# Stick-breaking attention: weights copied by a transfer within SBUF into rounded float32 tiles and transposed in that format

## Chip, cores and metric

The kernel runs on one core of a Trainium2 chip. The metric is the device time of one execution in microseconds (us); the number given for a kernel is the median of its runs.

## What is computed

One decoder layer over 1024 tokens of width 1024: a modulated RMS norm, one input projection, two attention families side by side (a sparse one with compressed, selected and windowed keys, and a stick-breaking one), their gated merge with an output projection, and a squared-ReLU MLP. The change lies in the stick-breaking family alone. It has 8 heads of width 64, no softmax, and is strictly causal:

```python
z = einsum('bqhd,bshd->bhqs', qb, k) * scale
mask = key_pos[None, :] < t[:, None]
log_keep = where(mask, log_sigmoid(-z), 0.0)
suffix = cumsum(log_keep, axis=3, reverse=True) - log_keep
a = where(mask, exp(log_sigmoid(z) + suffix), 0.0)
out = einsum('bhqs,bshd->bqhd', a, v)
```

So a weight is sigmoid(z) times the product of sigmoid(-z) over all keys between it and the query.

## The kernel before

The layer runs in stages on one core: norm and first projections, sparse attention, stick-breaking attention, the up-projections with merge and output projection, then the MLP. Products that need accuracy are split in a high and a low part in the rounded float32 format (F32R), and the parts are multiplied apart. All matrices that the attention stages leave room for are multiplied inside them: `fill_all` (L1044) yields the matmuls of 28 units of the input projection (L761, 128 x 512 each), and `drive` (L1067) lets the attention code, written as generators, run and puts in fill matmuls by an estimated cost. `behind` (L746) ties every sixth fill matmul behind the last attention matmul. 96 fill matmuls are kept back (`TAIL`, L1042) and run right after the stick-breaking stage. The final order on each engine is made by a scheduler from this program order. All transfers of the stage are issued by one engine, SP, in order.

`sb_gens` (L1089) is the stick-breaking stage. For each of 8 heads there are three groups of four blocks (`chunks_of`, L1140): kind 0 are the query rows 0 to 3 (of 128 queries each) with keys up to the diagonal, 512, 384, 256 and 128 wide; kind 1 rows 4 to 7 with the last 512 keys; kind 2 the same rows with the keys before those, again 512, 384, 256 and 128 wide. That makes 96 blocks.

- `sb_a` (L1148) computes a block's scores on TensorE (PE) in a PSUM bank of a ring of three (`psx`, L1156 to L1159), then two sigmoids on ScalarE (ACT): sigmoid(z) into an SBUF tile (`sig` by width, two of each, or `sigr` for kind 1, five; L1160, L1161), sigmoid(-z) in place in the bank (L1162). Its second half `fin` runs the products from the right by a scan on VectorE (DVE) into `Pt` (L1171) and multiplies `sig` with them on GpSimd (POOL, L1173).
- `turn` (L1180) transposes the finished weights on PE, up to four 128 x 128 pieces from up to four tiles into one bank of a ring of two (`pt`, L1188). In the program text a group's turns stand beside the next group's scores; the scheduler lets the scores run up to three groups ahead.
- `halves` (L1192) splits the transposed bank: the high part by a copy on ACT (`th`, L1196), the low part by a subtraction on DVE (`tl`, L1197).
- `times_v` (L1200) multiplies both with the head's value rows into one bank (`po`, L1208). At the end of a row group the two halves are added and stored (`osum`, L1214, and L1215 by SP).
- `prep` (L1104) splits the next head's keys and queries, mostly on POOL in pieces of 1 to 2.4 us; `prep_v` (L1120) transposes value rows (L1126) for two heads at a time.
- Beside all that, one step of another matrix, `ada_rest` (L427), runs on ACT and POOL after every second block in the first heads: a load by SP (L436), a scaling on ACT (L456) and an addition on POOL (L460).

The sparse stage already has the step that the change brings here: `scaler` (L910) scales a block on POOL, SP copies it into an F32R tile `Pr` (L926, L927), and L975 transposes from there with the F32R identity `identr`.

Of the kernel before, what the change touches and what calls it, by code (L numbers as in the profile page):

```python
# [6 lines left out]
F32 = mybir.dt.float32  # L7
F32R = mybir.dt.float32r
# [7 lines left out]
S = 1024  # L16
# [19 lines left out]
def build(tc, I, out):  # L36
    nc = tc.nc
    opened = []

    def pool(name, side=None, bufs=1, **kw):  # L40
        if side:
            kw.update(side=side, reuse_waits="tile")
        p = tc.alloc_tile_pool(name=name, bufs=bufs, **kw)
        opened.append(p)
        return p
# [9 lines left out]
    f = lambda t: t.bitcast(F32)  # L55
# [29 lines left out]
    z_d = dr.tile([28, 128, S], F32, name="z_d")  # L85
# [11 lines left out]
    def psx(name="psx"):  # L97
        return ps.tile([128, 512], F32, tag="s", bufs=3, name=name)

    def pt(name="pt"):  # L100
        return ps.tile([128, 512], F32, tag="t", bufs=2, name=name)
# [6 lines left out]
    ident = const.tile([128, 128], F32, name="ident")  # L108
# [633 lines left out]
    def track(ins):  # L742

        last[:] = [ins.ins]
# [29 lines left out]
    identr = wu.tile([128, 128], F32R, name="identr")  # L774
# [314 lines left out]
    def sb_gens(sp):  # L1089
# [7 lines left out]
            return zr  # L1097

        def load_v(p):
            vr = sp.tile([128, S], F32, name="vr", bufs=1)  # L1100
            nc.sync.dma_start(vr, z_d[8 + p])
            return vr

        def prep(h, ld):  # L1104
# [15 lines left out]
        def prep_v(vr, V):  # L1120
            tv = [sp.tile([128, NT, 2, HD], F32R, name="V", bufs=3) for _ in range(2)]
            for q in range(2):
                p = pt()
                for c in range(4):
                    kt = q * 4 + c
                    track(nc.tensor.transpose(p[:, c * 128:(c + 1) * 128], vr[:, kt * 128:(kt + 1) * 128], ident))  # L1126
                yield 4 * PT_
                pv_ = p.rearrange("p (c h d) -> p c h d", c=4, h=2)
                for j in range(2):
                    nc.scalar.copy(tv[j][:, q * 4:q * 4 + 4, 0], pv_[:, :, j])  # L1130
                for j in range(2):
                    nc.vector.tensor_tensor(tv[j][:, q * 4:q * 4 + 4, 1], pv_[:, :, j],
                                            f(tv[j])[:, q * 4:q * 4 + 4, 0], op=OP.subtract)
                yield 0.0
            V.extend(tv)
# [12 lines left out]
        def sb_a(kind, chunk, ops, A, edges):  # L1148

            i, c0, c1 = chunk  # L1150
            Q, Kh, Kl = ops
            w = c1 - c0
            p = psx()
            qs = Q[:, i * 128:(i + 1) * 128]
            diag = kind != 2
            track(nc.tensor.matmul(p[:, :w], qs, Kh[:, c0:c1], start=True, stop=False))  # L1156
            track(nc.tensor.matmul(p[:, :w], qs, Kl[:, c0:c1], start=False, stop=not diag))
            if diag:
                track(nc.tensor.matmul(p[:, w - 128:w], identr, diagr, start=False, stop=True))  # L1159
            sig = sp.tile([128, w], F32, name="sigr" if kind == 1 else "sig%d" % w, bufs=5 if kind == 1 else 2)  # L1160
            nc.scalar.activation(sig, p[:, :w], AF.Sigmoid, scale=HD ** -0.5)  # L1161
            nc.scalar.activation(p[:, :w], p[:, :w], AF.Sigmoid, scale=-(HD ** -0.5))  # L1162
            A[i, kind] = (sig, c0)

            def fin():
                Pt = sp.tile([128, 640], F32, name="Pt", bufs=6)
                if diag:
                    nc.vector.memset(Pt[:, w:w + 1], 1.0)
                else:
                    nc.vector.tensor_copy(Pt[:, w:w + 1], edges.pop(i)[:, 0:1])  # L1170
                nc.vector.tensor_tensor_scan(Pt[:, 0:w][:, ::-1], p[:, 0:w][:, ::-1], zero.to_broadcast([128, w]),  # L1171
                                             1.0 if diag else Pt[:, w:w + 1], op0=OP.mult, op1=OP.add)
                nc.gpsimd.tensor_tensor(sig, sig, Pt[:, 1:w + 1], op=OP.mult)  # L1173
                if kind == 1:
                    edges[i] = Pt
            return fin, max(w, 256) * 2 / 2400.
# [3 lines left out]
        def turn(h, g, kt, A):  # L1180

            p = pt()
            c0 = max(0, kt - 4 * g) * 128
            for i in range(max(4 * g, kt), 4 * g + 4):
                o = (i - 4 * g) * 128
                sig, s0 = [A[i, x] for x in ((0,) if g == 0 else (1, 2)) if (i, x) in A and
                           A[i, x][1] <= kt * 128 < A[i, x][1] + A[i, x][0].shape[1]][0]
                track(nc.tensor.transpose(p[:, o:o + 128], sig[:, kt * 128 - s0:kt * 128 - s0 + 128], ident))  # L1188
            turned.append((h, g, kt, c0, p))
            return (512 - c0) / 128. * PT_  # L1190

# [26 lines left out]
        def sb_all():  # L1218
            lds = {0: (load(0, 0), load(4, 0))}
            vr = load_v(0)  # L1220
            ops = {}
            for r in prep(0, lds[0]):
                ops[0] = r
            V = []
            for c in prep_v(vr, V):
                yield c
# [3 lines left out]
            for k in range(len(groups) + 1):  # L1230
                if k < len(groups):
                    h, kind = groups[k]
                    if kind == 0:
                        A[h, 0] = {}
                        if h + 1 < 8:
                            lds[h + 1] = (load((h + 1) // 2, h + 1), load(4 + (h + 1) // 2, h + 1))
                            if h % 2 == 1:
                                vr = load_v((h + 1) // 2)
                    if kind == 1:
                        A[h, 1] = {}  # L1240
                        if h + 1 < 8:
                            extra.append(prep(h + 1, lds[h + 1]))
                            if h % 2 == 1:
                                extra.append(prep_v(vr, V))
                    chunks = chunks_of(kind)
                for c in range(4):
                    cost = 0.0
                    if k < len(groups):
                        fin, cost = sb_a(kind, chunks[c], ops[h], A[h, min(kind, 1)], edges)
                        late.append(fin)  # L1250
                        yield cost
# [4 lines left out]
                    if k > 0:  # L1256
                        hb, kb = groups[k - 1]
                        g = min(kb, 1)
                        cost += turn(hb, g, (3, 7, 3)[kb] - c, A[hb, g])

                        if split_ and (wait[0] or split_[0][2] != 4 * split_[0][1] + 3):
                            while len(split_) > 0:
                                cost += times_v(V)
                            wait[0] = 0
                        elif split_:
                            wait[0] = 1
                        if len(turned) > 1:
                            halves()
# [62 lines left out]
    def col_sums(r, bank):  # L1331
        acc = L["wr"].tile([128, D], F32, name="raw", bufs=3)
        nc.sync.dma_start(acc, acc_d[r])
        p = bank()
        for j in range(NK):
            nc.tensor.matmul(p[:, j:j + 1], acc[:, j * 128:(j + 1) * 128], ones[:, 0:1], start=True, stop=True)
        return p
# [43 lines left out]
    sp = pool("sb", "right")  # L1381
# [49 lines left out]
    for n in range(len(units) + lag):  # L1431
        if n < len(units):
            ma[n] = up_unit(0, n)
        if n >= lag:
            d, th = units[n - lag]
# [7 lines left out]
        if n == 8:  # L1443
            p = col_sums(1, px)
            nc.vector.tensor_tensor(s2, p[:, :NK], cols[:, 24:32], op=OP.add)
        if n == 10:
            p = col_sums(2, px)
# [146 lines left out]
    A, SPL, U = {}, {}, {}  # L1594
# [199 lines left out]
```

## Time and profile before

| | |
|---|---|
| median of 3 runs (lowest to highest) | 1703.29 us (1702.85 to 1706.73) |
| the profiled execution: its own time | 1704.85 us |
| the profiled execution: span, first to last instruction | 1703.1 us |
| mean granted TensorE clock | 0.989 of 2.4 GHz |
| PE busy | 1636.8 us, 96% |
| DVE busy | 1273.8 us, 75% |
| POOL busy | 950.7 us, 56% |
| ACT busy | 873.9 us, 51% |
| DMA, SP's hardware queue | 276.13 MB, 48.8% of 16 engines' span |

The profile shows one execution. Busy time is the time in which an engine had an instruction in work; the ends of PE's pipelined matmuls are modelled, so successive matmuls overlap in the rows and the distance of their starts is the better measure. The chain is followed back from the last instruction: at each step to what released it, or to the instruction before it on its engine. A wait is named by who waited, and for whom.

### The profile page before, as it was taken

To read this page: it belongs to the slowest core of one execution; us is meant where nothing else is said; L and a number is where in the kernel's file an instruction comes from. 1 tells how busy PE (TensorE), PEld (TensorE's weight loads), DVE (VectorE), ACT (ScalarE), POOL (GpSimd) and SP (SyncE) were. 2 spreads that over 40 slices of the span, in tenths; PEclk is the share of its full clock that TensorE was granted. 3 is DMA by queue.
4 is the path that set the end of the run, shared out by engine and by line. 5 is a ranking of instruction groups with operands and counts; after the bars stand their busy time and mean duration, and the time that the engine had idled before them with its cause. 6 is when DMAs were issued, how large, how long until landed. Compare 5 with 4: busy or idle time off the path is not lost.

```text
span 1703.1 us, 25878 instructions
## 1 busy us (share of the span) xinstructions
PE 1636.8 (96%) x8484; PEld 1377.4 (81%) x8484; DVE 1273.8 (75%) x2614; ACT 873.9 (51%) x1898; POOL 950.7 (56%) x837
## 2 busy tenths in 40 slices
PE   6999999999999989999999999989999999999998
PEld 5879888888888867878778887768788888888886
DVE  7698478778777557878655557569888888979897
ACT  6433476667666456766554435534444443454442
POOL 0021143434434268775326303399889897989897
PEclk9999999999999999999999999999999999999999
DMA  9465344444543474441187543855363554636232
GB/s 304 109 198 157 110 142 156 128 149 143 166 131 125 130 196 128 115 125 59 36 301 232 165 151 127 292 212 210 134 262 116 231 211 148 251 113 268 98 148 99
DMA packets 195103, 279.87 MB, mean 164 GB/s; under 512 B 19401, under 2 KB 145049, under 8 KB 186009
## 3 DMA queue, kind: packets, MB, share of 16 engines
q1 hardware_dynamic: 190744, 276.13, 48.8%
q10 hardware_dynamic: 4224, 2.10, 0.4%
q8 instruction: 67, 1.10, 0.3%
q14 instruction: 68, 0.55, 0.1%
HBM read 203.71 MB, written 39.86 MB: 143 GB/s over the span
## 4 chain that ended last, share of the span: by engine, by line
PE 73%; POOL 8%; DMA 6%; DVE 6%; issue 3%; ACT 3%; SPq 1%; POOLq 0%; DVEq 0%; ACTq 0%
PE pd L761 15%; PE psx L1734 10%; PE pd L1668 7%; PE pt L1668 5%; PE px L1357 5%; PE po L955 4%; PE px L1470 4%; PE po L1734 3%; POOL raw L1708 3%; PE pt L975 2%; PE psx L844 2%; DMA adraw<-in_ada_w_dram 2%; PE psx L845 2%; POOL wbl L1710 1%; PE psx L603 1%
## 5 line engine op out<-in xcount | busy, mean ns | idle before, releaser
L1737 DVE TENSOR_TENSOR acc<-acc,psx 128x512 f32<-128x512 f32 x288 | 178.7, 675 | 9.8 <-PE psx L1734 9.7
L761 PE MATMUL pd<-uh,uwh 128*128 128x512 f32 x448 | 181.2, 404 | 0.7 <-ACT zo L1051 0.7
L761 PE MATMUL pd<-ul,uwh 128*128 128x512 f32 x448 | 177.4, 396 | 0.0
L761 PE MATMUL pd<-uh,uwl 128*128 128x512 f32 x448 | 177.1, 395 | 0.0
L66 DVE TENSOR_TENSOR wl<-aw,wh 128x1024 fp32r<-128x1024 f32 x49 | 114.6, 2339 | 63.9 <-ACT wh L61 63.9
L1708 POOL TENSOR_TENSOR raw<-r 128x512 f32<-128x512 f32 x80 | 132.5, 1675 | 32.1 <-ACT r L1643 32.0
L1734 PE MATMUL psx<-wbl,rah 128*128 128x512 f32 x336 | 131.3, 391 | 5.9 <-POOL wbl L1710 4.6
L1734 PE MATMUL psx<-wbh,rah 128*128 128x512 f32 x336 | 130.6, 390 | 1.9 <-ACT wbh L1709 1.5
L1734 PE MATMUL psx<-wbh,ral 128*128 128x512 f32 x336 | 130.9, 390 | 0.1
L947 DVE TENSOR_TENSOR tl<-pt,th 128x512 fp32r<-128x512 f32 (+8 forms) x168 | 103.5, 619 | 32.9 <-ACT th L946 31.4
L946 ACT CAST th<-pt 128x512 fp32r<-128x512 f32 (+8 forms) x168 | 88.9, 533 | 68.2 <-PE pt L975 67.0
L1710 POOL TENSOR_TENSOR wbl<-raw,wbh 128x1024 fp32r<-128x1024 f32 x40 | 108.9, 2724 | 19.5 <-ACT wbh L1709 19.5
L63 POOL TENSOR_SCALAR uwh<-uwr 128x512 fp32r<-128x512 f32 x54 | 34.3, 645 | 136.0 <-PE pd L761 115.9
L1696 POOL TENSOR_TENSOR w<-w,grow 128x1024 f32<-128x1024 f32 x32 | 95.0, 2992 | 11.8 <-DVE aw L1624 11.8
L1709 ACT CAST rah<-raw 128x1024 fp32r<-128x1024 f32 x40 | 41.5, 1051 | 113.9 <-PE po L1734 60.7
L761 PEld LDWEIGHTS pd<-uh,uwl 128*128 128x128 f32 x448 | 84.9, 189 | 17.2
L761 PEld LDWEIGHTS pd<-uh,uwh 128*128 128x128 f32 x448 | 85.2, 190 | 14.9 <-ACT zo L1051 1.1
L901 POOL TENSOR_TENSOR pcx<-pcx,tot 128x64 f32<-128x64 f32 (+7 forms) x32 | 11.5, 359 | 153.5 <-ACT Pn L864 40.8
L761 PEld LDWEIGHTS pd<-ul,uwh 128*128 128x128 f32 x448 | 85.1, 190 | 14.0
L1668 PE MATMUL pd<-mth,wh 128*128 128x512 f32 x224 | 87.3, 390 | 0.9 <-ACT wh L61 0.9
L1668 PE MATMUL pd<-mth,wl 128*128 128x512 f32 x224 | 87.1, 389 | 0.9 <-DVE wl L66 0.9
L1668 PE MATMUL pd<-mtl,wh 128*128 128x512 f32 x224 | 87.2, 389 | 0.0
(359 smaller groups left out, 5326.3 us busy)
## 6 DMA issues: line engine op xcount, KB each, us to landing
mtl<-t_d SPq DMA_DIRECT2D x35, 1024.0 KB, 5.7
mth<-t_d SPq DMA_DIRECT2D x35, 1024.0 KB, 8.2
w<-in_mlp_w_dram SPq DMA_DIRECT2D x32, 512.0 KB, 5.5
z_d<-zo SPq DMA_DIRECT2D x56, 256.0 KB, 2.3
Pr<-Pn SPq DMA_DIRECT2D x112, 128.0 KB, 2.0
aw<-in_mlp_w_dram SPq DMA_DIRECT2D x28, 512.0 KB, 4.0
uwr<-in_w_in_dram SPq DMA_DIRECT2D x54, 256.0 KB, 3.2
adraw<-in_ada_w_dram SPq DMA_DIRECT2D x48, 256.0 KB, 3.1
```

The lines of the kernel that those rows point to most:

```text
L66: (nc.vector if e == "v" else nc.gpsimd).tensor_tensor(dst, src, f(h), op=OP.subtract)
L761: r = nc.tensor.matmul(p, a, b, start=(k == 0 and n == 0), stop=(k == NK - 1 and n == 2))
L946: nc.scalar.copy(th[:rows, :w], p[:rows, :w])
L947: nc.vector.tensor_tensor(tl[:rows, :w], p[:rows, :w], f(th)[:rows, :w], op=OP.subtract)
L955: track(nc.tensor.matmul(po_[:, :256], w, tt[q][:rows, m * 256:(m + 1) * 256], start=(n == 0 and m == 0 and q == 0), stop=(n == last and m ...
L1357: nc.tensor.matmul(p, a, b, start=(k == 0 and n == 0), stop=(k == 3 and n == 2))
L1668: nc.tensor.matmul(bank[ft], a[:, k, fs], b[k], start=(k == 0 and m == 0 and not on), stop=(k == 3 and m == 2), skip_group_check=on)
L1696: nc.gpsimd.tensor_tensor(W2[c][j], W2[c][j], grow2, op=OP.mult)
L1708: nc.gpsimd.tensor_tensor(d, block(i0, j0, s), block(i1, j1, s), op=OP.add if sg > 0 else OP.subtract)
L1710: (nc.vector if e == "v" else nc.gpsimd).tensor_tensor(l.rearrange("p s n -> p (s n)"), src, f(h).rearrange("p s n -> p (s n)"), op=OP.sub ...
L1734: nc.tensor.matmul(p, a[:, s, qs], b[:, s], start=(s == 0 and n == 0), stop=(s == 1 and n == 2))
L1737: nc.vector.tensor_tensor(acc[:, t, ds_], acc[:, t, ds_], p, op=OP.add if sg > 0 else OP.subtract)
```

## The change

The product of `sig` and `Pt` is still made by POOL in place, but `sig` is now one ring of four tiles for all widths. SP then copies each product, bit for bit, into an F32R tile (`Sr` by width, two of each, or `Sr` for kind 1, five), and `turn` transposes from that tile with `identr`. Value rows are loaded into a tile that is declared F32R and are transposed in that format too. The stage gets 96 transfers within SBUF; 288 transposes of weights and 32 of values change their format.

```diff
--- before.py
+++ after.py
@@ -1097,8 +1097,8 @@
             return zr
 
         def load_v(p):
-            vr = sp.tile([128, S], F32, name="vr", bufs=1)
-            nc.sync.dma_start(vr, z_d[8 + p])
+            vr = sp.tile([128, S], F32R, name="vr", bufs=1)
+            nc.sync.dma_start(f(vr), z_d[8 + p])
             return vr
 
         def prep(h, ld):
@@ -1123,7 +1123,8 @@
                 p = pt()
                 for c in range(4):
                     kt = q * 4 + c
-                    track(nc.tensor.transpose(p[:, c * 128:(c + 1) * 128], vr[:, kt * 128:(kt + 1) * 128], ident))
+                    track(nc.tensor.transpose(p[:, c * 128:(c + 1) * 128].bitcast(F32R),
+                                              vr[:, kt * 128:(kt + 1) * 128], identr))
                 yield 4 * PT_
                 pv_ = p.rearrange("p (c h d) -> p c h d", c=4, h=2)
                 for j in range(2):
@@ -1157,10 +1158,12 @@
             track(nc.tensor.matmul(p[:, :w], qs, Kl[:, c0:c1], start=False, stop=not diag))
             if diag:
                 track(nc.tensor.matmul(p[:, w - 128:w], identr, diagr, start=False, stop=True))
-            sig = sp.tile([128, w], F32, name="sigr" if kind == 1 else "sig%d" % w, bufs=5 if kind == 1 else 2)
+            sig = sp.tile([128, 512], F32, name="sig", bufs=4)[:, :w]
             nc.scalar.activation(sig, p[:, :w], AF.Sigmoid, scale=HD ** -0.5)
             nc.scalar.activation(p[:, :w], p[:, :w], AF.Sigmoid, scale=-(HD ** -0.5))
-            A[i, kind] = (sig, c0)
+
+            turned_ = sp.tile([128, w], F32R, name="Sr" if kind == 1 else "Sr%d" % w, bufs=5 if kind == 1 else 2)
+            A[i, kind] = (turned_, c0)
 
             def fin():
                 Pt = sp.tile([128, 640], F32, name="Pt", bufs=6)
@@ -1171,6 +1174,7 @@
                 nc.vector.tensor_tensor_scan(Pt[:, 0:w][:, ::-1], p[:, 0:w][:, ::-1], zero.to_broadcast([128, w]),
                                              1.0 if diag else Pt[:, w:w + 1], op0=OP.mult, op1=OP.add)
                 nc.gpsimd.tensor_tensor(sig, sig, Pt[:, 1:w + 1], op=OP.mult)
+                nc.sync.dma_start(f(turned_), sig)
                 if kind == 1:
                     edges[i] = Pt
             return fin, max(w, 256) * 2 / 2400.
@@ -1185,7 +1189,7 @@
                 o = (i - 4 * g) * 128
                 sig, s0 = [A[i, x] for x in ((0,) if g == 0 else (1, 2)) if (i, x) in A and
                            A[i, x][1] <= kt * 128 < A[i, x][1] + A[i, x][0].shape[1]][0]
-                track(nc.tensor.transpose(p[:, o:o + 128], sig[:, kt * 128 - s0:kt * 128 - s0 + 128], ident))
+                track(nc.tensor.transpose(p[:, o:o + 128].bitcast(F32R), sig[:, kt * 128 - s0:kt * 128 - s0 + 128], identr))
             turned.append((h, g, kt, c0, p))
             return (512 - c0) / 128. * PT_
```

The change also moves instructions inside the stage, since the scheduler orders them anew; after the stage's last transpose, the order on all engines is as before. Two places are shown. The first is PE's order where head 4's scores begin (heads count from 0), among the transposes of head 3: the last turn of one of its groups, with four weight tiles, and the first of the next group. `psx<-Kh,Q` and `psx<-Kl,Q` are a block's scores, `pt<-ident` a transposition, `po<-th,V` and `po<-tl,V` the product with the values. Before:

```order
L761 MATMUL pd<-uh,uwl 128x512
L1208 MATMUL po<-th,V 128x384
L1188 MATMUL pt<-ident,sig_10081 128x128
L1188 MATMUL pt<-ident,sig_10055 128x128
L1188 MATMUL pt<-ident,sig_10024 128x128
L1188 MATMUL pt<-ident,sig_9993 128x128
L1208 MATMUL po<-tl,V 128x384
L1188 MATMUL pt<-ident,sigr 128x128
L1156 MATMUL psx<-Kh,Q 128x128
L1157 MATMUL psx<-Kl,Q 128x128
L1159 MATMUL psx<-diagr,identr 128x128
L1208 MATMUL po<-th,V 128x512
```

And now the same place:

```order
L761 MATMUL pd<-uh,uwl 128x512
L1157 MATMUL psx<-Kh,Q 128x384
L1158 MATMUL psx<-Kl,Q 128x384
L1160 MATMUL psx<-diagr,identr 128x128
L1212 MATMUL po<-th,V 128x384
L1192 MATMUL pt<-identr,Sr_10161 128x128
L1192 MATMUL pt<-identr,Sr_10133 128x128
L1192 MATMUL pt<-identr,Sr_10100 128x128
L1192 MATMUL pt<-identr,Sr_10067 128x128
L1212 MATMUL po<-tl,V 128x384
L1192 MATMUL pt<-identr,Sr 128x128
L1157 MATMUL psx<-Kh,Q 128x256
```

Of the next head's scores, the block of 384 columns has moved ahead of the run of five transposes; before, the first scores behind that run were those of the 128-wide block.

The second place is SP's queue while the first head's last group of blocks is under way, where the new transfers (`Sr<-sig`) stand among the loads and stores. Before:

```order
L436 DMA adraw<-in_ada_w_dram 128x256
L1215 DMA ob_d<-osum 64x512
L436 DMA adraw<-in_ada_w_dram 128x256
L464 DMA acc_d<-adacc 128x256
L1052 DMA z_d<-zo 128x512
L1096 DMA zr<-z_d 64x1024
L436 DMA adraw<-in_ada_w_dram 128x256
L1096 DMA zr<-z_d 64x1024 x3
L436 DMA adraw<-in_ada_w_dram 128x256
L723 DMA uwr<-in_w_in_dram 128x4x128
```

And now:

```order
L1177 DMA Sr<-sig 128x512 x3
L436 DMA adraw<-in_ada_w_dram 128x256
L464 DMA acc_d<-adacc 128x256
L1177 DMA Sr_9129<-sig 128x512
L1219 DMA ob_d<-osum 64x512
L1177 DMA Sr_9157<-sig 128x384
L436 DMA adraw<-in_ada_w_dram 128x256
L1096 DMA zr<-z_d 64x1024
L1052 DMA z_d<-zo 128x512
L1177 DMA Sr_9191<-sig 128x256
L1096 DMA zr<-z_d 64x1024 x2
L1177 DMA Sr_9215<-sig 128x128
```

Between two transfers there is at one point a store of a finished output (`ob_d<-osum`), at others a load for the next head (`zr`), of the side matrix (`adraw`) or a store of the fill (`z_d<-zo`).

## Rows read from the trace of the kernel before

**Rows 1.** The page, chain that ended last: share of the span by engine.
```profile
PE 73%; POOL 8%; DMA 6%; DVE 6%; issue 3%; ACT 3%; SPq 1%; POOLq 0%; DVEq 0%; ACTq 0%
```

**Rows 2.** Line L1188: ns min/median/max, first and last start.
```profile
L1188 PE MATMUL pt<-ident,sig x160: 270/272/476, 627.3 to 845.5; 128*128 128x128 f32 x160
...
L1188 PE MATMUL pt<-ident,sigr x128: 270/272/421, 638.1 to 843.2; 128*128 128x128 f32 x128
```

**Rows 3.** Windows: engines' busy us (instructions), granted clock, DMA share, GB/s.
```profile
400.00:560.00 160.00, 156.40 (x1030) 139.15 (x1029) 123.28 (x479) 103.93 (x331) 62.16 (x129) 0.99 0.43 138
620.00:640.00 20.00, 15.13 (x68) 12.63 (x69) 15.80 (x28) 16.82 (x39) 16.72 (x19) 0.79 0.49 137
680.00:700.00 20.00, 18.06 (x96) 15.20 (x95) 14.03 (x27) 14.46 (x33) 15.37 (x16) 0.91 0.34 97
613.00:846.00 233.00, 216.32 (x1170) 179.89 (x1168) 175.60 (x338) 159.43 (x366) 156.28 (x163) 0.97 0.38 102
```

**Rows 4.** Waits of 613 to 846 us: who waited for whom, us, times, longest.
```profile
PE psx L1156 <- DVE Pt L1171: 11.0, 8, 4.7
...
ACT sig L1161 <- PE pt L1188: 13.2, 10, 3.1
...
ACT sigr L1161 <- PE pt L1188: 4.3, 8, 0.8
```

**Rows 5.** Timeline of ACT and PE at two of the four stretches; idle before in brackets.
```profile
668.13 0.38 ACT L1161 ACTIVATE sig<-psx 128x256 f32<-128x256 f32 x1 [0.85 <-PE pt L1188]
...
669.56 0.33 PE L1156 MATMUL psx<-Kh,Q 128*128 128x128 f32 x1 [0.96 <-DVE Pt L1171]
...
828.39 0.33 PE L1156 MATMUL psx<-Kh,Q 128*128 128x128 f32 x1 [0.56 <-DVE Pt L1171]
```

**Rows 6.** Timeline of PE: start us, us, instruction; float32 transposes, then rounded ones.
```profile
794.64 0.38 PE L1188 MATMUL pt<-ident,sigr 128*128 128x128 f32 x2
794.86 0.38 PE L1188 MATMUL pt<-ident,sig 128*128 128x128 f32 x2
...
795.31 0.40 PE L761 MATMUL pd<-uh,uwh 128*128 128x512 f32 x1
795.54 0.40 PE L761 MATMUL pd<-ul,uwh 128*128 128x512 f32 x1
...
454.87 0.46 PE L975 MATMUL pt<-identr,Pr 128*128 128x128 f32 x4
...
455.35 0.28 PE L955 MATMUL po<-th,vS 128*128 128x256 f32 x1
455.47 0.28 PE L955 MATMUL po<-tl,vS 128*128 128x256 f32 x1
```

**Rows 7.** Tile Pr of the sparse stage: SP's issue times (ns) and landing times.
```profile
L927 SPq DMA_DIRECT2D Pr<-Pn x128: 464/541/1845, 220.0 to 576.6; - x128
...
DMA to landing us min/median/max: 1.8/2.0/3.9
```

**Rows 8.** Timeline of POOL and PE: first and last 512-wide product, the latter's transpose.
```profile
623.25 1.09 POOL L1173 TENSOR_TENSOR sig<-sig,Pt 128x512 f32<-128x512 f32 x1 [0.80 <-ACT adraw L456]
...
831.31 1.46 POOL L1173 TENSOR_TENSOR sig<-sig,Pt 128x512 f32<-128x512 f32 x2 [0.97 <-DVE Pt L1171]
...
840.37 0.27 PE L1188 MATMUL pt<-ident,sig 128*128 128x128 f32 x1
```

**Rows 9.** Timeline of POOL and ACT near 700 us: products, and ACT's first sigmoid of a block.
```profile
700.48 2.89 POOL L1173 TENSOR_TENSOR sig<-sig,Pt 128x256 f32<-128x256 f32 x4
...
700.93 0.64 ACT L1161 ACTIVATE sigr<-psx 128x512 f32<-128x512 f32 x1
```

**Rows 10.** Lines by form, 600 to 860 us: the 512-wide scan; busy us, mean ns, idle.
```profile
L1171 DVE TENSOR_TENSOR_SCAN Pt<-psx,zero 128x512 f32<-128x512 f32 x40 | 48.7, 1220 | 13.7 <-ACT psx L1162 13.6
```

**Rows 11.** Waits of SP's queue, 600 to 850 us: us in total, times, longest.
```profile
SPq L1215 <- DVE osum L1214: 31.3, 6, 11.9
...
SPq L1215 <- DVE Pt L1170: 16.1, 3, 7.5
```

## The prediction

> **What bounds the kernel now.** I read the page first: PE holds 73% of the chain that ended last [rows 1]. So PE is the engine to relieve, if the relief falls where PE is what others wait for. The change touches the stick-breaking stage alone; its first and last weight transposes start at 627.3 and 845.5 us [rows 2], and I take 613 to 846 us as the stage. Over these 233 us the windows show PE busy 216.32, DVE 175.60, ACT 159.43 and POOL 156.28 us [rows 3]: PE leads, but by 17%, and DVE is next. The ends of matmuls are modelled, so the waits must say where PE really stood. They say: PE's largest wait is 11.0 us in 8 pieces for the scan (L1171), that is for a free score bank, and ACT waited 13.2 + 4.3 us for transposes before it could write a new sigmoid tile [rows 4].
>
> The second wait leads to the first. The program order (section on the change) has, at a head's start, four or five transposes and only then the next scores. In the trace ACT's sigmoid of a 256-wide block is released by the transposes at 668.13, the scan follows, and PE stands idle for 0.96 us until 669.56; the same picture returns twice and a last time at 828.39 with 0.56 us [rows 5]. Four such stretches come to some 3.5 us. There PE releases ACT late and pays for it itself.
>
> **The cost of each part.** *Transposes in the rounded format.* 160 + 128 of weights change [rows 2], and 32 of values. Durations of matmuls overlap, so I take starts; the stage before this one, sparse attention, already turns its weights in the rounded format. Four float32 transposes and one 512-wide matmul need 794.64 to 795.31 = 0.67 us; such a matmul alone 795.31 to 795.54 = 0.23; so the four cost 0.44. Four in the rounded format and a 256-wide matmul need 454.87 to 455.35 = 0.48 us; the matmul 0.12; so 0.36 [rows 6]. That is 0.08 per four, 20 ns each, and 320 x 20 ns = 6.4 us. PE is busy in 216.32 of 233 us, 93%, so I count **6 us** as gained; the ends are 0 (it falls into PE's waits) and 6.4.
>
> By the Trainium skill (TensorE: Matmul & The Clock Gate, section "Back-to-back issue gap") a steady stream of weight load and 128-column matmul comes to about 81 ns a pair. An estimate by that figure would be a saving of 29 ns each, 9.3 us in all; the row's four at 0.36 us are 90 ns each, so the measurement decides and the sum keeps 20 ns.
>
> *The tile that ACT writes becomes free earlier.* Before, it was held until its transposes; now until a transfer has copied it. The wait of 17.5 us on ACT goes. Its worth on PE is the four idle stretches, **3.5 us** (0.96 to 0.56 each) [rows 5]. Nothing is the lower end; the upper is all of PE's waits for the scan but the first, 11.0 - 4.7 = 6.3 us [rows 4], since that first one stands before any weight is turned. What is late next there is the scan itself, on DVE.
>
> *96 transfers within SBUF.* The nearest row is the same step of the sparse-attention stage: 464 to 541 ns on SP's queue at the minimum and median, 1.8 to 3.9 us to landing, median 2.0 [rows 7]. On SP that is 96 x 0.54 = 52 us of a 233 us stage, beside waits, and nothing else needs SP that often. On the weights' way it adds about 0.5 + 2.0 = 2.5 us between the product and its transpose. Cover: the first product ends at 623.25 + 1.09 = 624.34 [rows 8] and its transpose starts at 627.3 [rows 2], 3 us later; the last 512-wide one is the first of the two that start at 831.31, so it ends near 832.4, and is turned at 840.37, 8 us later [rows 8]. Between these two, product and transpose stand further apart in the program order, since scores run two to three groups of four ahead of the transposes. So I cost the latency at nothing; only the first group has no margin. In the new order of PE the scores run less far ahead in the first heads, six to ten blocks in place of some twelve, but that is still more than a group of four, and four blocks take 4 x 233/96 = 9.7 us. If that cover went, each group of four would lose up to 2.5 us, 24 groups 60 us.
>
> *The smaller ring.* Thirteen tiles that ACT wrote become four. A 512-wide block occupies one for its two sigmoids (0.64, and as much again, overlapped: some 1.1), scan (1.22), product (1.09) and transfer (2.5): 5.9 us [rows 7 to 10], while blocks come every 2.43 us, four of them in 9.7 us. On the average that holds; it fails where POOL is late behind its own preparation of the next head. At 700.93 ACT starts a block whose ring predecessor, four blocks before, is the first of the four products that start at 700.48 and take 2.89 us together [rows 9]; with some 0.6 us for it and 2.5 for its transfer the new rule makes ACT wait until 703.6, 2.7 us. I expect this about once per head, and behind ACT wait the copies of turned weights (L1196), so PE follows in part: from 0 to 8 x 2.7 = 22 us. PE has fill matmuls of 0.23 us, six to twelve of them per group, to run meanwhile, so I take the near end, **2.5 us**.
>
> *Moved work on SP.* SP issues in order. The new order puts stores of finished outputs (L1215 before), loads of a later weight matrix (L436) and of the fill (L723) between the transfers. Before, SP waited 31.3 + 16.1 us in 9 pieces for such an output, the longest 11.9 [rows 11]; now a transfer may stand behind. I cost it at nothing in the sum, since the cover above is 8 us or more behind the first group, and it makes the rival below.
>
> **Sum:** -6 - 3.5 + 2.5 = -7.0 us against the profiled execution's 1704.85 us gives 1697.85. That execution is 1.56 us above the median of the three runs (1703.29), so I forecast **1696.3**. After the stage the order of all engines is unchanged, with 96 fill matmuls first, so what is won passes on.
>
> **The rivals.**
> *More is won:* no ring wait, and every scan wait goes: -6.4 - 6.3 = -12.7, 1690.6. For it: ACT is busy 68% only. Against: DVE at 75% has to feed PE faster.
> *Hidden:* PE's shorter transposes only lengthen its waits, because scan, copy and subtraction on DVE set a head's pace. For it: the four stretches of [rows 5] were ended by DVE. Or the rounded format costs the same here. It leaves the four stretches' half, -2 us: 1701.
> *Slower, through SP:* a store waits for its output, a transfer stands behind, the ring of four runs dry and ACT stops, and with it the copy that the output itself needs next. It decides from a store's wait above 9.7 - 5.9 = 3.8 us. The mean in [rows 11] is 47.4/9 = 5.3, so 1.5 us over for each of 16 stores, 24 us on ACT; if PE feels half, +12, less 6 won: +6, 1709. Against: cover of 8 us and more.
> *Slower, through the clock:* the granted clock was 0.79 on the mean at 620 to 640 us, behind a PE wait of 4.7 us, and 0.91 at 680 to 700 [rows 3, 4], so a short fall cost 9% of 20 us, 1.8 us. If the lighter transposes let it fall so once more in each of eight heads, that is +14.4, less 7: +7.4, 1710.7. Against: with rounded transposes all along, 400 to 560 us was granted 0.99 [rows 3]. The Trainium skill (same page, section "Part 4: PE-mode transpose") says that transposes don't count as busy for the clock gate; the 0.99 of that stretch does not show harm from them.
>
> **How the numbers follow.** A measurement of this kernel can tell about 0.3%, 5.1 us, from no change: the bounds are 1698.2 and 1708.4. Forecast case 0.45 (1692 to 1700; three quarters of it, 0.34, under 1698.2), more won 0.12, hidden 0.25, SP 0.13, clock 0.05. Faster: 0.34 + 0.12 = 0.46. Same: 0.11 + 0.25 = 0.36. Slower: 0.18. The range 1690 to 1708 takes in the first three cases and leaves out nearly all of the two slower ones, which hold 0.18.
>
> **What would show it.** Right: four rounded weight transposes near 0.36 us from start to start; no wait of ACT's sigmoid for transposes; PE's wait for the scan under 8 us; DVE's busy time the same in a shorter stage. The ring shows as ACT's sigmoid waiting for the transfer, under 10 us in all. Wrong: PE waiting for the transfer, SP's waits for outputs followed by late transfers, or a granted clock under 0.95 in the stage after 640 us.

## The result: slower, with the profile after

The changed kernel takes 1718.12 us at the median of four runs (1714.49 to 1721.9), the kernel before, beside it, 1704.57 us (1702.85 to 1706.73). The ratio is 1.0075, 95% interval 1.0052 to 1.0099: 12.8 us slower, outside the predicted range and of the other sign. The profiled execution took 1714.49 us, 9.6 more than that of before (1704.85). Its last weight transpose starts at 854.9 us, before at 845.5 [rows 2]: 9.4 us of the 9.6 are lost by the end of the stick-breaking stage.

In the experiments below a time stands beside that of the kernel before, run with it: between 1703.97 and 1705.68 us at the median. One execution each of experiments 3 and 13 was disturbed and does not enter the ratios; in experiment 3 it is the profiled one, so none of its rows are used.

First the page of the changed kernel: the chain's shares (answers to [rows 1]) and the busy times.

```profile
PE 1638.3 (96%) x8484; PEld 1372.5 (80%) x8484; DVE 1271.4 (74%) x2614; ACT 873.2 (51%) x1898; POOL 951.9 (56%) x837
...
PE 70%; POOL 8%; DMA 8%; DVE 6%; issue 4%; ACT 3%; SPq 1%; POOLq 0%; DVEq 0%; ACTq 0%
```

PE gave up three points of the chain, and DMA gained two, issue one. In the chain's part from 613 to 855 us the new transfers hold 16.2%, and PE's fill matmuls (L761) fell from 29.4% to 17.0%: transfers now stand on the path. The same windows as [rows 3] (busy us of PE, PEld, DVE, ACT and POOL, granted clock, DMA share, GB/s), the stage now 9 us longer:

```profile
613.00:855.00 242.00, 219.54 (x1154) 177.68 (x1152) 172.98 (x338) 158.05 (x365) 156.89 (x162) 0.95 0.58 175
620.00:640.00 20.00, 17.00 (x66) 12.83 (x67) 15.05 (x28) 13.98 (x34) 15.31 (x18) 0.78 0.71 220
660.00:680.00 20.00, 18.45 (x98) 15.15 (x97) 14.15 (x34) 13.39 (x34) 15.44 (x15) 0.91 0.69 212
680.00:700.00 20.00, 18.39 (x95) 15.12 (x93) 16.08 (x31) 15.49 (x36) 15.58 (x17) 0.91 0.67 209
720.00:740.00 20.00, 18.56 (x101) 15.29 (x99) 14.80 (x34) 13.07 (x33) 16.78 (x17) 0.91 0.74 216
780.00:800.00 20.00, 18.34 (x93) 14.72 (x93) 12.44 (x32) 11.09 (x28) 11.63 (x12) 0.91 0.29 99
```

PE was idle for 242 - 219.54 = 22.5 us, before for 233 - 216.32 = 16.7. DVE, ACT and POOL have as much work as before in a longer stage, so none of them became the bound by its own load. The granted clock is 0.95 in place of 0.97. It shows 0.91 in four windows; before, 680 to 700 us did [rows 3]. The waits of 613 to 855 us, as in [rows 4], say who stood:

```profile
POOL sig L1176 <- DVE Pt L1174: 50.5, 38, 5.4
...
DVE Pt L1174 <- ACT psx L1163: 28.2, 24, 3.5
DVE tl L1201 <- ACT th L1200: 26.9, 22, 4.7
ACT sig L1162 <- DMA Sr<-sig: 25.9, 19, 5.5
...
PE psx L1157 <- DVE Pt L1174: 13.8, 16, 5.3
```

ACT's wait for transposes (17.5 us) is gone, as predicted, and a wait of 25.9 us for the transfer stands in its place. PE's wait for the scan went from 11.0 us in 8 pieces to 13.8 in 16. The longest of ACT's waits, in the timelines of POOL, SP, ACT and PE (start us, us, instruction, idle before it and what ended that), with one row of the chain, the transfer from its issue to its landing:

```profile
757.58 2.40 POOL L66 TENSOR_TENSOR Kl<-zr,Kh 128x1024 fp32r<-128x1024 f32 x1
760.06 2.37 POOL L1113 TENSOR_TENSOR Q<-zr,Q 64x1024 fp32r<-64x1024 f32 x1
762.51 2.89 POOL L1176 TENSOR_TENSOR sig<-sig,Pt 128x128 f32<-128x128 f32 x4
...
763.00 0.55 SPq L1177 DMA_DIRECT2D Sr<-sig  x1
...
763.00 4.51 DMA Sr<-sig
...
767.87 0.28 ACT L1162 ACTIVATE sig<-psx 128x128 f32<-128x128 f32 x1 [5.52 <-DMA Sr<-sig]
...
768.83 0.50 PE L1157 MATMUL psx<-Kh,Q 128*128 128x512 f32 x1 [0.89 <-DVE Pt L1174]
```

POOL prepares the next head for almost 5 us and then makes four products. ACT waits for the transfer of the first of them, the block four before its own. SP issues it at 763.00 us, as soon as that product is made, but it takes 4.51 us to land, and only then may ACT write again: 5.52 us. Right behind, PE stands 0.89 us for a scan.

The transposes did become shorter. In PE's timeline (answers to [rows 6]) four of them and a 512-wide matmul need 708.99 - 708.39 = 0.60 us, less 0.23 for the matmul: 0.37, predicted 0.36, before 0.44.

```profile
708.39 0.46 PE L1192 MATMUL pt<-identr,Sr 128*128 128x128 f32 x4
708.68 0.46 PE L1212 MATMUL po<-tl,V 128*128 128x512 f32 x1
708.99 0.39 PE L761 MATMUL pd<-uh,uwh 128*128 128x512 f32 x1
```

The transfers' issue is as priced, too. They land after 2.4 us at the median, where 2.0 had been read, and after 5.6 at the most, where 3.9 had [rows 7]. The tile's view (issue on SP in ns, landing in us, transposes):

```profile
L1192 PE MATMUL pt<-identr,Sr x288: 218/248/369, 625.8 to 854.9; 128*128 128x128 f32 x144
L1177 SPq DMA_DIRECT2D Sr<-sig x96: 464/482/1362, 622.6 to 840.3; - x96
...
DMA to landing us min/median/max: 1.8/2.4/5.6
```

So the single prices nearly held, and the sum did not. My first theory: **the ring of four**, whose tiles are now held through product, SP's queue and landing, stops ACT. Rivals: the transfers themselves (SP, DMA), the clock under lighter transposes, and later transposes.

### The profile page after: what moved, and what is told of

Its sections match the earlier page's. It is cut to its first block, busy times and chain, and to the rows that moved or that the text cites. A ratio compares the mean times of both kernels' runs of the same rounds, so it can differ in the third digit from the quotient of the medians.

```text
span 1712.8 us, 26216 instructions
## 1 busy us (share of the span) xinstructions
PE 1638.3 (96%) x8484; PEld 1372.5 (80%) x8484; DVE 1271.4 (74%) x2614; ACT 873.2 (51%) x1898; POOL 951.9 (56%) x837
## 4 chain that ended last, share of the span: by engine, by line
PE 70%; POOL 8%; DMA 8%; DVE 6%; issue 4%; ACT 3%; SPq 1%; POOLq 0%; DVEq 0%; ACTq 0%
PE pd L761 14%; PE psx L1738 10%; PE pd L1672 8%; PE pt L1672 5%; PE px L1361 5%; PE po L955 5%; PE px L1474 4%; PE po L1738 3%; POOL raw L1712 3%; PE pt L975 2%; DMA Sr<-sig 2%; PE px L1589 2%; PE psx L844 2%; PE psx L845 2%; POOL wbl L1714 1%
## 5 line engine op out<-in xcount | busy, mean ns | idle before, releaser
L761 PE MATMUL pd<-uh,uwh 128*128 128x512 f32 x448 | 182.9, 408 | 0.7 <-ACT zo L1051 0.7
L761 PE MATMUL pd<-ul,uwh 128*128 128x512 f32 x448 | 179.3, 400 | 0.0
L761 PE MATMUL pd<-uh,uwl 128*128 128x512 f32 x448 | 178.7, 399 | 0.0
L66 DVE TENSOR_TENSOR wl<-aw,wh 128x1024 fp32r<-128x1024 f32 x49 | 113.9, 2325 | 65.0 <-ACT wh L61 65.0
L1176 POOL TENSOR_TENSOR sig<-sig,Pt 128x512 f32<-128x512 f32 (+1 forms) x96 | 86.1, 904 | 57.8 <-DVE Pt L1174 50.5
L761 PEld LDWEIGHTS pd<-uh,uwl 128*128 128x128 f32 x448 | 85.9, 192 | 17.5
L761 PEld LDWEIGHTS pd<-uh,uwh 128*128 128x128 f32 x448 | 85.9, 192 | 15.2 <-ACT zo L1051 1.1
L761 PEld LDWEIGHTS pd<-ul,uwh 128*128 128x128 f32 x448 | 86.2, 192 | 14.1
```

What stands on the lines that cost most here:

```text
L66: (nc.vector if e == "v" else nc.gpsimd).tensor_tensor(dst, src, f(h), op=OP.subtract)
L761: r = nc.tensor.matmul(p, a, b, start=(k == 0 and n == 0), stop=(k == NK - 1 and n == 2))
```

## The experiments

**1. Eight tiles for ACT in place of four.**

```diff
-            sig = sp.tile([128, 512], F32, name="sig", bufs=4)[:, :w]
+            sig = sp.tile([128, 512], F32, name="sig", bufs=8)[:, :w]
```

> The changed kernel with eight sigmoid tiles in the ring in place of four; the transfers and the rounded format stay. Theory ring (four tiles, each held until its transfer has landed, stop ACT): ACT's sigmoids wait under 5 us for transfers in place of 25.9 us, and the time falls to 1696 to 1704 us. Theory clock (lighter transposes let the TensorE clock fall more often) and theory SP (transfers late behind other work on SP's queue): the time stays at 1714 to 1722 us and the granted clock falls as often in the stage.

Measured: 1712.56 us, 1.0052 [1.0037, 1.0068]: outside both ranges. At most a part of the loss came back, and the interval overlaps that of the changed kernel (1.0052 to 1.0099). In its waits ACT still stands for the transfer, and on SP's queue transfers now wait for a free target, that is for PE to turn an older weight:

```profile
ACT sig L1162 <- DMA Sr<-sig: 18.3, 15, 3.3
...
SPq L1177 <- PE pt L1192: 41.8, 24, 5.0
```

In the changed kernel this wait of SP was 12.3 us. A transfer that finds no target holds its source. So the two rings are coupled: a longer first one can run into the second.

**2. Transfers and rings, but float32 transposes.**

```diff
-            turned_ = sp.tile([128, w], F32R, name=...)
+            turned_ = sp.tile([128, w], F32, name=...)
...
-                nc.sync.dma_start(f(turned_), sig)
+                nc.sync.dma_start(turned_, sig)
...
-                track(nc.tensor.transpose(p[:, o:o + 128].bitcast(F32R), sig[...], identr))
+                track(nc.tensor.transpose(p[:, o:o + 128], sig[...], ident))
```

> The changed kernel with plain float32 destination tiles and float32 weight transposes: the transfers and the ring of four stay, the rounded format of the weights goes (value rows keep it). Ring: 5 to 6 us slower than the changed kernel, 1719 to 1726 us, with ACT again waiting over 20 us for transfers. Clock: near the kernel before, 1703 to 1708 us, with no more falls of the clock in the stage than there.

Measured: 1719.09 us, 1.0096 [1.0061, 1.0131], as slow as the changed kernel. The loss needs no rounded weight transposes. That speaks against the clock rival.

**3. The rings, no transfer: POOL rounds.**

```diff
-                nc.gpsimd.tensor_tensor(sig, sig, Pt[:, 1:w + 1], op=OP.mult)
-                nc.sync.dma_start(f(turned_), sig)
+                nc.gpsimd.tensor_tensor(turned_, sig, Pt[:, 1:w + 1], op=OP.mult)
```

> The changed kernel without the transfers: GpSimd writes its product straight into the rounded tile, so the weights are rounded once more; the ring of four stays but a tile is free when the product is made, 2.5 us earlier. Ring: ACT waits under 8 us for its ring and the time is 1696 to 1704 us. Clock: the lighter transposes are still there, so the time stays at 1712 to 1722 us. SP: 1696 to 1704 us as well, since nothing is queued.

Measured: 1704.49 us, 1.0001 [0.9988, 1.0014], half a microsecond above the ring's range and far under the clock's. The ring still has four tiles, but ACT's is free at the product, and the whole loss is gone. Here, without transfers, a ring of four is enough. Just as telling: no loss, rounded transposes, and still nothing gained.

**4. GpSimd issues the transfers.**

```diff
-                nc.sync.dma_start(f(turned_), sig)
+                nc.gpsimd.dma_start(f(turned_), sig)
```

> The changed kernel with the 96 transfers issued by GpSimd right after its product, in place of SP. SP theory: transfers no longer stand behind stores and loads, the ring is free in time and the time falls to 1698 to 1706 us. Ring theory: the transfer's own latency remains, GpSimd gets the issuing as well, and the time stays at 1712 us or rises up to 1735 us.

Measured: 1761.3 us, 1.0333 [1.0309, 1.0356], 43 us more than the changed kernel and above both ranges. By lines (busy us, mean ns), issuing takes POOL's own time, on the engine that makes the products:

```profile
L1177 POOL DMA_DIRECT2D Sr<-sig x96 | 55.0, 573 | 0.4 <-POOL sig L1176 0.4
```

Relieving SP won nothing that shows beside this. ACT's sigmoids still wait 17.3 us for transfers there (613 to 900 us), so a part of that wait does not come from SP's queue.

**5. The format alone:** the kernel before, its 13 tiles rounded, no transfer.

```diff
-            sig = sp.tile([128, w], F32, name="sigr" if kind == 1 else "sig%d" % w, bufs=5 if kind == 1 else 2)
+            sig = sp.tile([128, w], F32R, name="sigr" if kind == 1 else "sig%d" % w, bufs=5 if kind == 1 else 2)
...
-                nc.gpsimd.tensor_tensor(sig, sig, Pt[:, 1:w + 1], op=OP.mult)
+                nc.gpsimd.tensor_tensor(sig, f(sig), Pt[:, 1:w + 1], op=OP.mult)
...
-                track(nc.tensor.transpose(p[:, o:o + 128], sig[...], ident))
+                track(nc.tensor.transpose(p[:, o:o + 128].bitcast(F32R), sig[...], identr))
```

> The kernel before with its own thirteen sigmoid tiles declared in the rounded format and the weights transposed in it; no transfer, no new ring (ACT and GpSimd round what they write, so the weights are rounded more than in either kernel). If PE's shorter transposes count as the prediction's sum has it: 1697 to 1700 us. If they only lengthen PE's waits (rival hidden): 1703 to 1706 us.

Measured: 1707.04 us, 1.0018 [1.0001, 1.0035], just above the range of "hidden". The step that I counted at 6 us is worth nothing by itself. Its stage in the window (columns as above):

```profile
613.00:845.00 232.00, 212.98 (x1172) 176.78 (x1171) 175.36 (x338) 157.66 (x366) 156.78 (x164) 0.97 0.38 104
```

PE's waits there:

```profile
PE psx L1156 <- DVE Pt L1171: 10.0, 9, 5.3
...
PE pt L1188 <- DVE tl L1197: 4.3, 5, 1.5
```

And the line of the transposes (ns, first and last start):

```profile
L1188 PE MATMUL pt<-identr,sig x160: 218/248/258, 629.9 to 847.0; 128*128 128x128 f32 x160
```

PE is less busy, 212.98 us of 232 against 216.32 of 233, and idle for 19.0 us in place of 16.7, while the last transpose starts no earlier than before (847.0 against 845.5). It waits 10.0 us for the scan and 4.3 for the subtraction of low parts, both DVE's: what the format saves, PE spends behind DVE.

**6. Transfers beside the work:** the kernel before, plus 96 transfers of the product into tiles that nobody reads.

```diff
                 nc.gpsimd.tensor_tensor(sig, sig, Pt[:, 1:w + 1], op=OP.mult)
+                spare = sp.tile([128, 512], F32, name="spare", bufs=4)[:, :w]
+                nc.sync.dma_start(spare, sig)
```

> The kernel before with 96 added transfers of each product into spare tiles that nobody reads; transposes read the old tiles, in float32. SP theory (issuing and traffic delay the loads and stores): 1709 to 1720 us. Theory that only the dependence through the rings costs time: 1702 to 1707 us.

Measured: 1706.31 us, 1.0013 [1.0002, 1.0024], some 2 us. SP's issues and the traffic are nearly free here, with PE's order that of the kernel before but for a stretch of 20 instructions; that leaves what is held through the transfers, and the new order.

**7. More targets, eight and three.**

```diff
-... name="Sr" if kind == 1 else "Sr%d" % w, bufs=5 if kind == 1 else 2)
+... name="Sr" if kind == 1 else "Sr%d" % w, bufs=8 if kind == 1 else 3)
```

> The changed kernel with longer rings of transfer targets (eight in place of five, three of each width in place of two); the ring of four stays. If transfers that wait for a free target and hold up SP's queue are the cause: SP's wait for transposes falls under 3 us and the time to 1703 to 1710 us. If the ring of four alone is: 1713 to 1722 us.

Measured: 1717.13 us, 1.0072 [1.0051, 1.0093], no gain. SP no longer waits for targets, and ACT still waits 24.8 us: with four tiles, longer targets alone don't help.

**8. Both rings longer:** six tiles for ACT, targets six and three.

```diff
-            sig = sp.tile([128, 512], F32, name="sig", bufs=4)[:, :w]
+            sig = sp.tile([128, 512], F32, name="sig", bufs=6)[:, :w]
...
-... bufs=5 if kind == 1 else 2)
+... bufs=6 if kind == 1 else 3)
```

> The changed kernel with six sigmoid tiles, six targets for the wide kind and three of each other width. If both rings together are the cause: ACT waits under 8 us for transfers and the time is 1698 to 1706 us, under the 1712.6 us of eight sigmoid tiles. If the cause is another (the order that the scheduler makes, with scores far ahead of transposes): 1708 to 1716 us again.

Measured: 1710.66 us, 1.0046 [1.0024, 1.0068]; ACT waits 20.1 us. That is in the range that was set for the other cause, the scheduler's order, and ACT's wait is not under 8 us. Transfers wait 12.6 us for targets here, about as in the changed kernel (12.3), so the targets alone do not keep ACT waiting. More tiles seem to narrow the loss, though the intervals of experiments 1, 7 and 8 all overlap that of the changed kernel; they don't close it.

**9. Three tiles.**

```diff
-            sig = sp.tile([128, 512], F32, name="sig", bufs=4)[:, :w]
+            sig = sp.tile([128, 512], F32, name="sig", bufs=3)[:, :w]
```

> The changed kernel with three sigmoid tiles in place of four: the suspected wait made larger. Ring theory: three blocks at the stage's 2.4 us per block, 7.3 us, hardly cover the 5.9 us hold, so ACT waits 40 us or more for transfers and the time rises to 1728 to 1760 us. If the ring is not what costs time: 1714 to 1722 us.

Measured: 1721.67 us, 1.0090 [1.0059, 1.0121], in the range for "not the ring" and not clear of the changed kernel's 1.0075. The waits, over 612 to 870 us:

```profile
ACT sig L1162 <- DMA Sr<-sig: 35.4, 28, 2.5
...
PE psx L1157 <- DVE Pt L1174: 17.4, 15, 5.3
...
SPq L1177 <- POOL sig L1176: 71.3, 50, 4.7
```

ACT's wait grows by 9.5 us and the median by 3.6, which the intervals don't tell from nothing. So most of an added wait may stay covered, and this run does not size the ring's cost.

**10. Another tile for the product:** ACT's ring of four is freed by the multiplication, and a second ring of four is held through the transfer.

```diff
-                nc.gpsimd.tensor_tensor(sig, sig, Pt[:, 1:w + 1], op=OP.mult)
-                nc.sync.dma_start(f(turned_), sig)
+                prod = sp.tile([128, 512], F32, name="prod", bufs=4)[:, :w]
+                nc.gpsimd.tensor_tensor(prod, sig, Pt[:, 1:w + 1], op=OP.mult)
+                nc.sync.dma_start(f(turned_), prod)
```

> The changed kernel with the product in a ring of four tiles of its own, transferred from there: ACT's ring of four is free when GpSimd has multiplied, and only GpSimd can wait for a transfer. Ring theory: ACT's waits for transfers go, and the time falls to 1703 to 1710 us. If transfers held up in SP's queue are the cause whoever waits for them: 1712 to 1720 us, with GpSimd waiting for transfers.

Measured: 1704.7 us, 1.0000 [0.9984, 1.0016]. The whole loss is gone, with all 96 transfers and all rounded transposes in place. With experiment 3 it decides whose tile must not be held. Its waits:

```profile
POOL prod L1177 <- DMA Sr<-prod: 40.0, 14, 8.5
...
PE psx L1157 <- DVE Pt L1174: 11.4, 8, 5.8
```

Its window, and below it the transposes:

```profile
613.00:845.00 232.00, 213.87 (x1171) 177.57 (x1171) 172.59 (x339) 159.40 (x368) 155.97 (x163) 0.96 0.61 184
```

```profile
L1193 PE MATMUL pt<-identr,Sr x288: 218/248/308, 630.3 to 843.0; 128*128 128x128 f32 x144
```

The wait hasn't vanished; it moved from ACT to POOL and grew to 40.0 us. There it costs nothing: PE's wait for the scan is back at 11.4 us in 8 pieces. One rival is left: the edits also make the scheduler order the stage anew. On PE, the places that differ between this kernel and the changed one span 1012 of 8484 instructions, so order and ring changed together, and no run changes the order alone. Against it, this kernel and experiment 3 have two different orders, and neither loses.

**11. More tiles in the kernel before,** eight and four.

```diff
-            sig = sp.tile([128, w], F32, name="sigr" if kind == 1 else "sig%d" % w, bufs=5 if kind == 1 else 2)
+            sig = sp.tile([128, w], F32, name="sigr" if kind == 1 else "sig%d" % w, bufs=8 if kind == 1 else 4)
```

> The kernel before with more sigmoid tiles (eight in place of five, four of each width in place of two), float32 transposes and no transfer: the prediction's second term alone. If ACT's wait for transposes cost PE its four idle stretches: 1698 to 1701 us. If something else ends those stretches anyway: 1702 to 1707 us.

Measured: 1705.64 us, 1.0004 [0.9988, 1.002]. ACT's wait for transposes fell from 17.5 us to 3.4 + 6.8, and PE's for the scan, 11.9, did not fall. More free tiles for ACT are worth nothing here.

**12. DVE relieved on the path:** the kernel before without the subtraction of low parts.

```diff
-            tl = sp.tile([128, 512], F32R, name="tl", bufs=4)
...
-            nc.vector.tensor_tensor(tl[:, c0:], p[:, c0:], f(th)[:, c0:], op=OP.subtract)
-            split_.append((h, g, kt, c0, th, tl))
+            split_.append((h, g, kt, c0, th, th))
```

> The kernel before without the 96 subtractions on DVE that make the low part of a turned weight (52 us of DVE): the high part is multiplied twice in its place, so PE's work stays and the result lacks the low part. If the chain through DVE sets the stage's pace and so hides what PE saves: PE's idle falls and the time by 10 us or more, to 1685 to 1695 us. If PE's own work, fill included, sets it: 1700 to 1705 us.

Measured: 1690.93 us, 0.9921 [0.9898, 0.9945], 13 us faster with float32 transposes and as many matmuls (the high part counts twice in its result, which is not the layer's).

```profile
613.00:846.00 233.00, 220.74 (x1223) 187.79 (x1222) 139.05 (x248) 162.60 (x372) 155.92 (x163) 0.99 0.40 113
```

In the same 233 us PE does 1223 matmuls that the profile records in place of 1170 [rows 3]. Its idle time is 233 - 220.74 = 12.3 us in place of 16.7, and the granted clock 0.99 in place of 0.97, so the gain is not idle time alone. PE's own load was not what set the stage's length; PE stood behind the chain through DVE. The run takes the subtraction off DVE and out of that chain at once, and does not tell the two apart.

**13. DVE relieved off the path:** the low parts of the fill's weights (L66) go to GpSimd in this stage.

```diff
-        lo(wl[:, 0:4], raw[0], wh[:, 0:4], "v")
+        lo(wl[:, 0:4], raw[0], wh[:, 0:4], low_on[0])
...
+    low_on = ["v"]
...
+    low_on[0] = "g"
     ...
+    low_on[0] = "v"
```

> The kernel before with the fill's 22 low-part subtractions of the stage (L66, 23.8 us on DVE, not in the attention's chain) on GpSimd. If DVE's load as a whole sets the pace that hides PE's gain: 1694 to 1700 us. If only the steps of the attention's own chain count (the subtraction that run 12 left out): 1701 to 1707 us, or more where GpSimd's products come later.

Measured: 1704.79 us, 1.0000 [0.9985, 1.0016]. DVE's busy time, before 175.60 us of 233 [rows 3], is 161.26 of 232, and nothing follows. From 600 to 860 us 16 of the subtractions run on GpSimd and 4 still on DVE, so DVE is relieved of some 14 us, against the 52 us of experiment 12. So much work of DVE that nobody waits for costs nothing.

**14. Experiments 10 and 13 in one kernel.** The edit is the sum of the two.

> Run 10 (rounded transposes, transfers from a ring of GpSimd's own) with the fill's low parts on GpSimd as well. If DVE's load is the cover, PE's saving now counts: 1690 to 1697 us, under both kernels. If GpSimd's waits for transfers (40 us in run 10) now hold up the fill: 1704 to 1715 us.

Measured: 1699.96 us, 0.9968 [0.9951, 0.9986]: faster than both kernels, some 5 us under the one before and 18 under the changed one, though short of what was expected. Its waits:

```profile
POOL prod L1178 <- DMA Sr<-prod: 18.1, 8, 4.2
...
PE psx L1158 <- DVE Pt L1175: 9.0, 7, 5.0
```

And its window:

```profile
613.00:845.00 232.00, 215.33 (x1189) 178.43 (x1188) 163.61 (x326) 159.41 (x369) 172.69 (x181) 0.97 0.62 187
```

Each edit alone is worth nothing that shows, both together some 5 us. I read that as a part of PE's saving that counts once DVE is lighter. Whether the saving is that of the rounded transposes or of the earlier freed tile was not separated under the lighter DVE.

## Why the prediction was wrong

**"I take the near end, 2.5 us" (the smaller ring)** is the step that failed first, and that turned the sign. The mechanism was named, with its place (POOL late behind its preparation of the next head) and its check: ACT's sigmoid waiting for the transfer, under 10 us in all. It measured 25.9 us, above even the upper bound of 22, and 19 pieces where I had counted eight. Taking the ring off the transfer (experiment 10) gives back all of the loss, so the term was about +13 us, if the order has no part in it. Two things were wrong in it. The occupation, 5.9 us with 2.5 from the product to the landing, was too small. By the timelines of ACT, POOL and SP (for the 46 of 96 blocks whose landing the trace tells) a transfer lands 3.6 us after its product at the median and 8.5 at the most, since it can stand in SP's queue first. A tile is held for 8.5 us at the median, 13.9 at the most, while the starts of four blocks lie 9.2 us apart at the median. So there was hardly a margin at any block, not only once per head. And I let PE's fill matmuls cover nine tenths of the wait; of the 25.9 us, 12.8, about half, came through. I also left out that a transfer can wait for its target (12.3 us on SP here, 41.8 in experiment 1).

**"I count 6 us as gained" (the rounded transposes).** The price was right, 0.37 us for four where 0.36 was expected. But the lower end was the truth: experiments 3, 5 and 10 have these transposes, no loss, and no gain. The step was drawn from PE's busy share of 93%; a busy share does not say whether PE's work ends last. Experiment 12 says it: with DVE's chain lighter the kernel is 13 us faster although PE's load is the same. This is the rival "hidden", which I gave 0.25, and it holds for the kernels without the ring's wait.

**"The four idle stretches, 3.5 us" (ACT's freed tile).** Nothing, by experiment 11. The stretches were real, but ended by DVE; a freer ACT did not shorten PE's waits for the scan.

**The transfers, costed at nothing.** Nearly right: experiment 6 measures some 2 us.

**The rival through SP,** which I gave 0.13. Its outcome, a dry ring and ACT standing, came, and so, in part, did its cause, stores ahead of the transfers. One of ACT's waits, in the timelines of POOL, SP and ACT:

```profile
699.88 0.64 POOL L1176 TENSOR_TENSOR sig<-sig,Pt 128x256 f32<-128x256 f32 x1
...
702.97 0.33 SPq L1052 DMA_DIRECT2D z_d<-zo  x1
703.56 0.47 SPq L1219 DMA_DIRECT2D ob_d<-osum  x1
704.13 0.55 SPq L1177 DMA_DIRECT2D Sr<-sig  x1
...
706.28 0.38 ACT L1162 ACTIVATE sig<-psx 128x256 f32<-128x256 f32 x1 [2.21 <-DMA Sr<-sig]
```

The product is ready at 700.52 us. SP stands until 702.97 for a store of the fill, then stores a finished output, and issues the transfer 3.61 us after its product. By the timelines the transfer that ends ACT's wait was issued 1.06 to 3.63 us behind its product in 12 of the 19 pieces, 12.3 of the 25.9 us; in the other seven SP was not late by more than 0.83 us. SP's own waits in total (600 to 860 us):

```profile
SPq L1177 <- POOL sig L1176: 31.6, 35, 3.4
SPq L1219 <- DVE osum L1218: 17.0, 8, 5.6
...
SPq L1177 <- PE pt L1192: 12.3, 8, 4.8
```

Transfers wait for POOL's products and for targets. Stores of outputs wait less than before: with their rows of 7.5, 5.9 and 2.7 us it is 33.1 us, before 64.7 (beside the 47.4 us that the prediction counted in [rows 11], the view has rows of 15.7 and 1.6 for the same store, in 7 pieces; by all 16 the mean is 4.0 us and not 5.3). What such delays are worth by themselves experiment 10 shows: POOL's longest wait there, 8.5 us, ends behind a store of the fill that SP issued only at 785.00 us, and nothing is lost. So SP's order makes the hold longer, and whose tile is held decides what that costs.

**The rival through the clock.** After 640 us the 0.91 of one window before [rows 3] is found in four now, so there are three more falls of the kind that I priced at 1.8 us: some 5 of the profiled execution's 9.6 us pass through them (an estimate). But the transposes are not their cause. Experiment 10, with the same transposes, has 0.96 in the stage, 0.985 over its profiled execution (the changed kernel 0.988) and an unchanged time, and experiment 2 loses as much with float32 transposes. The Trainium skill (TensorE: Matmul & The Clock Gate, "Part 4: PE-mode transpose") says that transposes don't count as busy in the same way for the clock gate; no run here shows harm from a format that makes them shorter.

**What stays open.** How the 13 us divide between PE's idle time (+5.8 us in the stage) and work at the lower clock; whether the scheduler's new order has a part in them; how much of ACT's wait would go if SP issued each transfer at once; and how much of experiment 14's gain is the format's.

## What to carry to other kernels

Before a transfer is put between a producer and a consumer, see whose buffer is held until it lands: a tile of an engine that others wait for should be freed by the step before, and the wait be left to an engine with slack (here POOL: 40.0 us of waits that cost nothing). Count a ring's hold from the first write to the landing, with the queue and the tail, and the target's ring with it; which length would be enough here no run shows (six and eight tiles still lost). A saving on the busiest engine may count for nothing while it waits behind another: test that by taking work off that other engine's chain before paying for the saving.

## What was not expected of the hardware

A DMA issued by GpSimd held that engine for 573 ns, 55.0 us for 96 of them, and that kernel is 43 us slower than the changed one (experiment 4). On SP an issue has a similar length (median 482 ns), and 96 of them cost some 2 us (experiment 6). I take from it that the engine that is held counts, and not the length; the queue differs, too.

A copy within SBUF landed after 1.8 to 5.6 us, median 2.4, in the changed kernel, and the tail is there when nobody reads the target, too (experiment 6; us to landing):

```profile
DMA to landing us min/median/max: 1.9/2.6/6.3
```

A ring that is sized by the median meets that tail, as ACT did at 767 us.
